# Loading the first block in two parts: sixteen partitions, then the other 112

## Chip, cores, metric

The kernel runs on one core of one Trainium2 chip. The metric is the device time of a run in microseconds. All runs quoted were with a granted clock of 1.0 (full speed).

## The reference

```python
def reference(x):                 # x: float32 [64, 256, 8192], 536.87 MB
    return np.mean(x, axis=2)     # [64, 256]
```

Every element is read once and added once. 16384 means come out.

## The kernel before

The 16384 rows of 32 KB are taken in 64 blocks of 256. Each of the 128 partitions gets two neighbouring rows, so 64 KB of HBM that lie together. From here on, "a row" of a load means these 64 KB of one partition: one DMA engine moves them, and the trace has one record of 65,536 bytes for them. Three slots of SBUF (the core's on-chip memory) hold blocks in turn. SyncE issues all loads, VectorE sums a block. The last block is cut into pieces and shared with ScalarE. The first load's issue is moved by hand ahead of the kernel's opening barrier.

```python
slots = [nc.alloc_sbuf_tensor(f"xt{i}", [P, R, S], F32) for i in range(SLOTS)]   # P=128, R=2, S=8192, SLOTS=3
load_sem = [tc.alloc_semaphore(f"load{i}") for i in range(LOAD_SEMS)]            # 6

def load(dst, src, sem):
    ld = untracked(nc.sync.dma_start(out=dst, in_=src))
    ...
    ld.then_inc(sem, 16)
    return ld

def loaded(n, ins):
    ins._wait_ge(load_sem[n % LOAD_SEMS], 16 * (n // LOAD_SEMS + 1))

for n in range(LB):                       # 63 whole blocks
    xt = slots[n % SLOTS]
    ld = load(xt[:], x_v[n], load_sem[n % LOAD_SEMS])
    if n == 0:
        first = ld
    if n < LB - 1:
        loaded(n, dve_sum(res[:, :, n], xt[:]))
    ...                                   # the last of them is shared with ScalarE
...                                       # last block in pieces, transposes, stores
body_bb.instructions.remove(first.ins)    # the first load goes to the head block,
...                                       # before SyncE's drain
head_bb.instructions.insert(at, first.ins)
```

## Time and profile before

| | before |
|---|---|
| time, median of 5 | 1246.84 us (1246.76 to 1246.90) |
| span of the profiled run | 1245.2 us |
| first sum starts | 21.83 us |
| a block arrives every | 19.35 us |
| VectorE waits before its sums, in total | 153.3 us |
| HBM read over the span | 431 GB/s |

The load stream is the bound: the load queue's records fill 99.8% of the sixteen DMA engines' span, and VectorE waits for each block. The prediction below shows the lines that carry this.

### The profile page before, as it was taken

What the parts mean: (1) busy time and instruction counts of PE and PEld (TensorE: products, weight loads), DVE (VectorE), ACT (ScalarE), POOL (GpSimd) and SP (SyncE); (2) the same over time, 40 slices, a digit from 0 to 9 for tenths busy, and PEclk for the clock granted to TensorE, in tenths of its full rate; (3) what the DMA queues carried; (4) which work ended last, traced back from release to release, by engine and by line L of the source; (5) the groups of instructions that cost most, each with busy time, mean ns of one, the idle gap of its engine ahead of it and who ended that gap; (6) DMA issues with size and microseconds to landing.
All of it is one profiled execution on the core that took longest, in us unless ns stands there. A gap on an engine that the chain in (4) does not pass through costs nothing.

```text
span 1245.2 us, 227 instructions
## 1 busy us (share of the span) xinstructions
PE 0.9 (0%) x2; PEld 0.4 (0%) x2; DVE 1087.4 (87%) x79; ACT 16.5 (1%) x13; POOL 0.7 (0%) x6
## 2 busy tenths in 40 slices
PE   0000000000000000000000000000000000000000
PEld 0000000000000000000000000000000000000000
DVE  3898988989889889898898988989889898898898
ACT  0000000000000000000000000000000000000004
POOL 0000000000000000000000000000000000000000
DMA  9999999999999999999999999999999999999998
GB/s 438 417 425 438 438 438 438 434 408 438 438 438 438 438 438 432 411 438 438 438 438 438 438 415 427 438 438 438 438 438 436 406 438 438 438 438 438 438 429 348
DMA packets 10169, 536.95 MB, mean 431 GB/s; under 512 B 1145, under 2 KB 1464, under 8 KB 1720
## 3 DMA queue, kind: packets, MB, share of 16 engines
q1 hardware_dynamic: 10168, 536.94, 99.8%
q14 instruction: 1, 0.01, 0.0%
HBM read 536.87 MB, written 0.07 MB: 431 GB/s over the span
## 4 chain that ended last, share of the span: by engine, by line
DMA 70%; DVE 29%; SPq 0%; issue 0%; DVEq 0%
DMA xt<-in_x_dram 70%; DVE res L92 29%; DVE fin_in L92 0%; SPq L82 0%; DVE fin_in L98 0%; DVE fin_t L109 0%; DVEq L98 0%
## 5 line engine op out<-in xcount | busy, mean ns | idle before, releaser
L92 DVE TENSOR_REDUCE res<-xt 128x2 f32<-128x16384 f32 (+1 forms) x63 | 1076.4, 17086 | 153.3 <-DMA xt<-in_x_dram 153.3
L95 ACT ACT_TABLE_LOAD x1 | 1.3, 1283 | 1181.3 <-DVE res L92 1181.3
L95 ACT ACTIVATE xt<-xt 128x8192 f32<-128x8192 f32 (+5 forms) x6 | 14.7, 2443 | 43.9 <-DMA xt<-in_x_dram 43.7
L92 DVE TENSOR_REDUCE fin_in<-xt 128x1 f32<-128x256 f32 (+3 forms) x5 | 5.0, 1005 | 0.3 <-DMA xt<-in_x_dram 0.2
L92 DVE TENSOR_REDUCE head<-xt 128x1 f32<-128x4096 f32 x1 | 4.4, 4420 | 0.2 <-DMA xt<-in_x_dram 0.2
L153 PE MATMUL ps<-ident,res 128*63 128x128 f32 x2 | 0.9, 460 | 1230.4 <-ACT xt L95 1229.3
L95 ACT ACTIVATION_READ_ACCUMULATOR xt<-xt 128x1 f32 x6 | 1.1, 186 | 0.0
L72 DVE MEMSET fin<- 128x32 f32 x2 | 0.1, 85 | 0.9 <-PEq L230 0.9
L154 DVE TENSOR_SCALAR bulk<-ps 63x128 f32<-63x128 f32 x2 | 0.6, 278 | 0.4 <-PE ps L153 0.4
L153 PEld LDWEIGHTS ps<-ident,res 128*63 128x63 f32 x2 | 0.4, 180 | 1230.6 <-issue 1229.2
L98 DVE TENSOR_SCALAR_CACHE_REDUCE fin_in<-fin_in 128x265 f32<-128x265 f32 x1 | 0.4, 431 | 0.2 <-DVE fin_in L92 0.2
L109 DVE STREAM_TRANSPOSE fin_t<-fin 128x32 f32<-128x32 f32 x2 | 0.4, 212 | 0.1
L60 POOL TENSOR_SCALAR_AFFINE_SELECT ident<-ident 128x128 f32<-128x128 f32 x1 | 0.3, 295 | 0.1
L98 DVE TENSOR_SCALAR_CACHE_REDUCE head<-head 128x2 f32<-128x2 f32 x1 | 0.2, 156 | 0.1
L59 POOL MEMSET ident<- 128x128 f32 x1 | 0.2, 205 | 0.4 <-POOLq L230 0.4
L230 POOL MEMSET const-bfloat16-1.0<- 128x1 bf16 x1 | 0.1, 103 | 0.0
L230 POOL MEMSET const-uint8-127<- 128x1 uint8 x1 | 0.1, 103 | 0.0
L230 POOL MEMSET const-float32-0.0<- 128x1 f32 x1 | 0.1, 99 | 0.2 <-issue 0.2
L230 POOL MEMSET const-float32-1.0<- 128x1 f32 x1 | 0.1, 99 | 0.0
L98 DVE DVE_READ_ACCUMULATOR head<-head 128x1 f32 x1 | 0.1, 85 | 0.0
L98 DVE DVE_READ_ACCUMULATOR fin_in<-fin_in 128x1 f32 x1 | 0.1, 84 | 0.0
## 6 DMA issues: line engine op xcount, KB each, us to landing
xt<-in_x_dram SPq DMA_DIRECT2D x1, 4096.0 KB, 31.2
xt<-in_x_dram SPq DMA_DIRECT2D x1, 2048.0 KB, 35.7
xt<-in_x_dram SPq DMA_DIRECT2D x1, 1024.0 KB, 37.7
xt<-in_x_dram SPq DMA_DIRECT2D x63, 40.8
xt<-in_x_dram SPq DMA_DIRECT2D x1, 512.0 KB, 38.5
xt<-in_x_dram SPq DMA_DIRECT2D x1, 256.0 KB, 38.7
xt<-in_x_dram SPq DMA_DIRECT2D x1, 128.0 KB, 38.6
fin_in<-in_x_dram SPq DMA_DIRECT2D x1, 128.0 KB, 38.4
```

The costliest lines, as they stand in the source:

```text
L59: nc.gpsimd.memset(ident[:], 0.0)
L60: nc.gpsimd.affine_select(out=ident[:], in_=ident[:], compare_op=mybir.AluOpType.not_equal, fill=1.0, base=0, pattern=[[-1, P]], channel_m ...
L72: nc.vector.memset(fin[r][:], 0.0)
L92: return untracked(nc.vector.tensor_reduce(out=dst, in_=src, axis=X, op=ADD))
L95: return untracked(nc.scalar.activation(out=src, in_=src, func=COPY, accum_out=dst))
L98: return nc.vector.tensor_scalar(out=src, in0=src, scalar1=inv, scalar2=None, op0=mybir.AluOpType.mult, op1=ADD, accum_out=dst,)
L109: nc.vector.transpose(out=fin_t[r][:], in_=fin[r][:])
L153: nc.tensor.transpose(out=ps[:LB, :], in_=res[:, r, :], identity=ident[:])
L154: nc.vector.tensor_scalar_mul(out=bulk[:LB, :, r], in0=ps[:LB, :], scalar1=inv)
L230: nc = _bacc.Bacc("TRN2", target_bir_lowering=False, num_devices=1)
```

## The change

Its intent, a supposition: a first transfer of only sixteen rows (part one) would have one descriptor (an order to move one row) for each engine, so the engines might begin sooner than when 128 descriptors are made. The other 112 rows follow at once in a second transfer (part two).

```diff
+ENGINES = 16
...
     def loaded(n, ins):
-        ins._wait_ge(load_sem[n % LOAD_SEMS], 16 * (n // LOAD_SEMS + 1))
+        loads = n // LOAD_SEMS + 1 + (n % LOAD_SEMS == 0)
+        ins._wait_ge(load_sem[n % LOAD_SEMS], 16 * loads)
...
     for n in range(LB):
         xt = slots[n % SLOTS]
-        ld = load(xt[:], x_v[n], load_sem[n % LOAD_SEMS])
+        sem = load_sem[n % LOAD_SEMS]
         if n == 0:
-            first = ld
+            first = [
+                load(xt[a:b], x_v[n, a:b], sem) for a, b in ((0, ENGINES), (ENGINES, P))
+            ]
+        else:
+            load(xt[:], x_v[n], sem)
...
-    (move first.ins to the head block)
+    for ld in first:
+        (move ld.ins to the head block)
```

The last two hunks are cut: the same lines that moved one issue now move both.

More of the change, by code (lines that the diff above doesn't have):

```diff
@@ L173 @@
     head_bb, body_bb = nc.main_func.blocks[:2]
-    assert first.ins in body_bb.instructions
-    body_bb.instructions.remove(first.ins)
-    at = next(
-        i
-        for i, ins in enumerate(head_bb.instructions)
-        if ins.engine == first.ins.engine and isinstance(ins, mybir.InstDrain)
-    )
-    head_bb.instructions.insert(at, first.ins)
+    for ld in first:
+        assert ld.ins in body_bb.instructions
+        body_bb.instructions.remove(ld.ins)
+        at = next(
+            i
+            for i, ins in enumerate(head_bb.instructions)
+            if ins.engine == ld.ins.engine and isinstance(ins, mybir.InstDrain)
+        )
+        head_bb.instructions.insert(at, ld.ins)
     DVE = mybir.EngineType.DVE
```

## The prediction

> **What bounds the kernel now.** I read the page first: the busy rows by slice, the groups, and the chain that ended last.
>
> ```profile
> DVE  3898988989889889898898988989889898898898
> DMA  9999999999999999999999999999999999999998
> ...
> HBM read 536.87 MB, written 0.07 MB: 431 GB/s over the span
> ...
> DMA xt<-in_x_dram 70%; DVE res L92 29%; DVE fin_in L92 0%; SPq L82 0%; DVE fin_in L98 0%; DVE fin_t L109 0%; DVEq L98 0%
> ...
> L92 DVE TENSOR_REDUCE res<-xt 128x2 f32<-128x16384 f32 (+1 forms) x63 | 1076.4, 17086 | 153.3 <-DMA xt<-in_x_dram 153.3
> ```
>
> The DMA row is full in every slice and moves 431 GB/s on average. VectorE is busy 87%, and all of its idle time before the sums (153.3 us) is ended by a load. The chain gives VectorE 29%, but that is the way slots come free, not the bound. The timeline of VectorE shows it:
>
> ```profile
> 21.83 17.22 DVE L92 TENSOR_REDUCE res<-xt 128x2 f32<-128x16384 f32 x1 [20.80 <-DMA xt<-in_x_dram]
> 41.15 17.22 DVE L92 TENSOR_REDUCE res<-xt 128x2 f32<-128x16384 f32 x1 [2.10 <-DMA xt<-in_x_dram]
> 60.50 17.22 DVE L92 TENSOR_REDUCE res<-xt 128x2 f32<-128x16384 f32 x1 [2.13 <-DMA xt<-in_x_dram]
> ```
>
> A sum takes 17.22 us, a new block lands every 19.35 us (60.50 - 41.15), so VectorE waits 2.1 us each time. A block is 128 rows of 64 KB, 8.39 MB; over 19.35 us that is 433.6 GB/s. Divided over 16 engines, each engine carries 8 rows, one after the other, at 19.35 / 8 = 2.418 us a row; call this one row time. The third slot keeps them supplied: load 3 is issued when the first sum ends (21.83 + 17.22 = 39.05), while load 2 lands only at about 60.5. So there is a reserve of some 20 us, and the time is the sum of each engine's back-to-back rows: whatever delays the slowest engine in the first block moves the end by as much, and nothing later makes it up.
>
> Next the start, in fine windows (columns: window, its length, five engines' busy times, clock, DMA share, GB/s; a packet is counted wholly in the window in which it starts):
>
> ```profile
> 0.00:1.00 1.00, 0.00 (x0) 0.00 (x0) 0.10 (x2) 0.00 (x0) 0.39 (x5) 1.00 0.00 0
> 1.00:1.25 0.25, 0.00 (x0) 0.00 (x0) 0.03 (x1) 0.00 (x0) 0.18 (x2) 1.00 7.85 2621
> 1.25:1.50 0.25, 0.00 (x0) 0.00 (x0) 0.00 (x0) 0.00 (x0) 0.14 (x1) 1.00 3.83 1311
> 1.50:1.75 0.25, 0.00 (x0) 0.00 (x0) 0.00 (x0) 0.00 (x0) 0.00 (x0) 1.00 0.70 262
> 1.75:4.00 2.25, 0.00 (x0) 0.00 (x0) 0.00 (x0) 0.00 (x0) 0.00 (x0) 1.00 0.00 0
> 4.00:4.25 0.25, 0.00 (x0) 0.00 (x0) 0.00 (x0) 0.00 (x0) 0.00 (x0) 1.00 2.42 1049
> 4.25:4.50 0.25, 0.00 (x0) 0.00 (x0) 0.00 (x0) 0.00 (x0) 0.00 (x0) 1.00 6.65 2884
> 4.50:4.75 0.25, 0.00 (x0) 0.00 (x0) 0.00 (x0) 0.00 (x0) 0.00 (x0) 1.00 0.60 262
> ```
>
> 2621 GB/s for 0.25 us is 655 KB, ten rows of 65,536 bytes; then 5, then 1. The sixteen engines start their first rows between 1.0 and 1.75 us after the issue, staggered, and their second rows (4, 11 and 1) between 4.0 and 4.75. This stagger is what the change aims at. In the trace's packet records the first rows start from 1.05 to 1.68 us and end from 4.05 to 4.56; at the end of the run the sixteen parts of a load still land 0.36 us apart, so the stagger is carried to the end.
>
> [...] So 16 rows and 112 rows both use 16 engines, one and seven rows each. [...] all rows of the steady state take the same 2.418 us, 27.1 GB/s an engine. [...]
>
> **The change part by part.** *Added issue.* One more DMA on SyncE's queue; issues of the big loads take 0.33 to 0.44 us in the timeline. The second part is issued about 0.4 us after the first, its rows reach the engines at about 1.5 us, before any first row ends (4.05). Loads 1 and 2 are issued 0.4 us later but are wanted at 21 us. Cost on the path: 0. The waits stay single waits, for 32 instead of 16 on the first; VectorE, ScalarE and TensorE have the same rows in the same order.
>
> *Gain, as intended.* If the stagger comes from 128 descriptors being made one after the other, it shrinks from 0.6 us to about a tenth. At the end only the slowest engine counts, and the sixteen parts land within 0.36 us, so the gain is at most about 0.4 us, 0.03%.
>
> [...]
>
> [...]
>
> Sum for the slowest engine: 3 + 4 = 7 row times, 7 x 2.418 = +16.9 us, minus at most 0.4. Load 0 then lands at 21.8 + 16.9 = 38.7, its sum ends at 55.9 and releases load 3. The fastest engine pays only the 3 row times: it ends load 0 at 28.6 to 29 and runs out of loads 1 and 2 at about 67. So nothing starves, no second cost is added, and the shift is carried unchanged: 1246.84 + 16.9 = 1263.7 us.
>
> **The rivals.** *[...] (load only staggered less).* [...] Time 1246.4 to 1247.5. I give it 15%.
> *[...] only part one pays.* [...] Then only +7.25 us, 1254. I give it 15%.
> *Rows are dealt in turn (row 16 + e + 16j to engine e).* [...] 8 rounds of 4 row times instead of 8 of 1, up to +58 us if engines stay in step, +35 to +55 if they drift apart; around 1290. [...] 15%.
> *The late first block starves the queue.* The reserve of 20 us speaks against: with +16.9 us and engines 10 us apart, 11 us remain.
>
> **Range and chances.** Consecutive sevens get 55%, giving 1259 to 1268[...]. Weighing in the cheaper rivals, which share 30%, I set the point a little below the sum, at 1262.0 us (+1.2%). The range 1246.2 to 1271.0 leaves out the dealing in turn. Within 2% means up to 1271.8: same 0.82; slower 0.17 (the dealing in turn, and a little for worse sharing); faster 0.01, as the intended gain is 0.4 us.
>
> **What would show it.** In the changed kernel's fine windows, sixteen rows should start by about 1.2 us, and the second rows only at about 10 to 11 us: that shows part one. If they start at 4.0 to 4.5, [...] the prediction falls. Load 0 should land at about 38 us, and its parts some 10 us apart (28 to 38) instead of 0.4; [...] over 60 us dealing in turn. From the second block on, VectorE should wait 2.1 us before each sum and blocks should come each 19.35 us as before; a longer period or a changed wait would mean that the cost isn't confined to the first block.

What is cut at the marks said how rows are dealt to engines and which partitions slow one another; no trace of the kernel before showed it. Two terms of the sum are cut with it. The sum came to 7 row times, +16.9 us, so 1263.7 us: +3 row times (7.25 us) on every engine for part one and +4 (9.67 us) on the slowest for part two. "Consecutive sevens" is the supposition that an engine's seven rows of part two go to neighbouring partitions. The first two rivals: that it doesn't matter which partitions a transfer writes, and that part two costs nothing. The 4 row times for sixteen rows that the third rival names were assumed; e3 later measured 3.9.

## More of the kernel before

One more line of the page, the data moved in 40 equal slices of the span, will be compared with the changed kernel's:

```profile
GB/s 438 417 425 438 438 438 438 434 408 438 438 438 438 438 438 432 411 438 438 438 438 438 438 415 427 438 438 438 438 438 436 406 438 438 438 438 438 438 429 348
```

Only the last slice, which holds the tail, is clearly lower. The start costs so little that the first slice reads as full.

## The result

The changed kernel takes 1268.43 us (median of 5, 1267.93 to 1268.69) against 1246.84. The ratio is 1.0172, 95% interval 1.0158 to 1.0186. Ratios here are the mean time of one kernel's fast runs over that of the other's in the same rounds, so not quite the ratio of the medians. The change costs 21.6 us, 1.7%, just inside the 2% that counts as the same.

The page of the changed kernel, in the lines that answer to those of before:

```profile
DVE  0598988988988989889889889898898898898988
DMA  9999999999999999999999999999999999999998
GB/s 217 366 437 430 433 430 430 430 430 433 435 439 441 437 433 430 430 430 430 433 433 433 435 447 435 433 430 430 430 430 433 433 433 433 451 433 433 430 430 338
...
HBM read 536.87 MB, written 0.07 MB: 424 GB/s over the span
...
DMA xt<-in_x_dram 71%; DVE res L94 29%; SPq L83 0%; DVE fin_in L94 0%; DVE fin_in L100 0%; DVE fin_t L111 0%; DVEq L100 0%
...
L94 DVE TENSOR_REDUCE res<-xt 128x2 f32<-128x16384 f32 (+1 forms) x63 | 1076.4, 17086 | 174.4 <-DMA xt<-in_x_dram 174.4
```

The sums cost exactly what they did (1076.4 us). VectorE's wait for loads grew from 153.3 to 174.4 us, by 21.1, nearly the whole loss of 21.6. The loss sits in the first two slices: 217 and 366 GB/s where there were 438 and 417. Note the DMA row: it still shows 9 in those slices. From 15 to 40 us the DMA share is 1.02 (a record counts where it starts) at 252 GB/s; before, from 10 to 20 us, it was 0.97 at 419. So a slow row counts as busy like a fast one, and the DMA row can't tell them apart; the GB/s row can.

VectorE's timeline (start, length, operation, and in brackets the wait and what ended it):

```profile
43.93 17.22 DVE L94 TENSOR_REDUCE res<-xt 128x2 f32<-128x16384 f32 x1 [42.45 <-DMA xt<-in_x_dram]
63.27 17.22 DVE L94 TENSOR_REDUCE res<-xt 128x2 f32<-128x16384 f32 x1 [2.12 <-DMA xt<-in_x_dram]
82.62 17.22 DVE L94 TENSOR_REDUCE res<-xt 128x2 f32<-128x16384 f32 x1 [2.13 <-DMA xt<-in_x_dram]
```

The first sum starts at 43.93 instead of 21.83 us, 22.1 later. After that the rhythm is that of before: 19.35 us a block, a wait of 2.1 us. So one event in the first block moves everything behind it.

The start in fine windows (window, length, five engines' busy times, clock, DMA share, GB/s; a row of 65,536 bytes is counted where it starts):

```profile
1.00:1.25 0.25, 0.00 (x0) 0.00 (x0) 0.00 (x0) 0.00 (x0) 0.00 (x0) 1.00 12.77 1573
1.25:1.50 0.25, 0.00 (x0) 0.00 (x0) 0.12 (x2) 0.00 (x0) 0.20 (x1) 1.00 1.79 262
1.50:1.75 0.25, 0.00 (x0) 0.00 (x0) 0.00 (x0) 0.00 (x0) 0.21 (x1) 1.00 2.10 262
1.75:2.25 0.50, 0.00 (x0) 0.00 (x0) 0.00 (x0) 0.00 (x0) 0.09 (x1) 1.00 8.42 1049
2.25:8.00 5.75, 0.00 (x0) 0.00 (x0) 0.00 (x0) 0.00 (x0) 0.00 (x0) 1.00 0.00 0
8.00:9.00 1.00, 0.00 (x0) 0.00 (x0) 0.00 (x0) 0.00 (x0) 0.00 (x0) 1.00 0.39 66
9.00:10.00 1.00, 0.00 (x0) 0.00 (x0) 0.00 (x0) 0.00 (x0) 0.00 (x0) 1.00 2.51 459
10.00:11.00 1.00, 0.00 (x0) 0.00 (x0) 0.00 (x0) 0.00 (x0) 0.00 (x0) 1.00 2.69 524
```

6, 1, 1 and 8 rows start by 2.25 us; then nothing starts until 8 us, and the second rows (1, 7, 8) come between 8 and 11. Before, they came between 4.0 and 4.75. Two things follow. The first rows take 7.2 to 9.0 us instead of 2.8 to 3.3. And the stagger that the change wanted to shrink did not shrink: the first rows start from 1.03 to 2.05 us, against 1.05 to 1.68 before.

The trace's record of every row shows one DMA engine's work in a chain, as each row starts when the one before it ends. One typical engine and one of the two slowest, in us a row:

```
before, any engine       3.0 | 2.42 2.42 2.42 2.42 2.42 2.42 2.42 | load 1: 2.42 2.42 ...
after, typical engine    8.4 | 5.51 4.79 3.02 3.73 4.41 4.70 4.40 | load 1: 3.26 2.42 ...
after, one of two        8.3 | 5.43 4.79 4.74 3.77 4.55 4.64 4.78 | load 1: 2.77 2.42 ...
```

The first bar ends part one, the second part two. From load 1's second row on all is as before.

### The profile page after: what moved, and what is told of

Same layout as the page of the kernel before. It is cut to its first block, busy times and chain, and to the rows that moved or that the text cites. A ratio compares the mean times of both kernels' runs of the same rounds, so it can differ in the third digit from the quotient of the medians.

```text
span 1266.6 us, 228 instructions
## 1 busy us (share of the span) xinstructions
PE 0.9 (0%) x2; PEld 0.4 (0%) x2; DVE 1087.2 (86%) x79; ACT 16.4 (1%) x13; POOL 0.7 (0%) x6
## 4 chain that ended last, share of the span: by engine, by line
DMA 71%; DVE 29%; SPq 0%; issue 0%; DVEq 0%
DMA xt<-in_x_dram 71%; DVE res L94 29%; SPq L83 0%; DVE fin_in L94 0%; DVE fin_in L100 0%; DVE fin_t L111 0%; DVEq L100 0%
## 5 line engine op out<-in xcount | busy, mean ns | idle before, releaser
L94 DVE TENSOR_REDUCE res<-xt 128x2 f32<-128x16384 f32 (+1 forms) x63 | 1076.4, 17086 | 174.4 <-DMA xt<-in_x_dram 174.4
L97 ACT ACTIVATE xt<-xt 128x8192 f32<-128x8192 f32 (+5 forms) x6 | 14.6, 2441 | 43.9 <-DMA xt<-in_x_dram 43.7
L160 PE MATMUL ps<-ident,res 128*63 128x128 f32 x2 | 0.9, 458 | 1251.9 <-ACT xt L97 1250.8
```

What stands on the lines that cost most here:

```text
L94: return untracked(nc.vector.tensor_reduce(out=dst, in_=src, axis=X, op=ADD))
L97: return untracked(nc.scalar.activation(out=src, in_=src, func=COPY, accum_out=dst))
L160: nc.tensor.transpose(out=ps[:LB, :], in_=res[:, r, :], identity=ident[:])
```

## The experiments

Twelve kernels, all edits of the changed kernel's first block unless told otherwise. Each also has its semaphore count fitted to its number of transfers, which the cuts below leave out. "Loss" is the median less that of the kernel before on the same chip in the same rounds (1246.7 to 1246.9). Each median is of four or five runs, in e11, e12 and e13 of two. The theory that they test: rows written at the same time slow one another or not, depending on which partitions they go to; below, a "conflict" is such a slowing. Where a mark stands before a number and no rival is named, the number is this theory's. The rivals: the splitting itself costs (an issue, descriptors, semaphore increments); the cold start costs; the places in HBM cost.

| run | first block loaded as | time us | loss us | first sum at us |
|---|---|---|---|---|
| e1_columns | 2 x (128 partitions, half the columns) | 1247.00 | 0.2 | 21.82 |
| e2_swap | 112, then 16 | 1268.29 | 21.5 | 43.67 |
| e3_eight_near | 8 x 16 neighbours | 1302.36 | 55.6 | 77.43 |
| e4_eight_spread | 8 x 16, every eighth | 1268.30 | 21.5 | 43.50 |
| e5_halves | 64, then 64 | 1267.96 | 21.3 | 43.31 |
| e11_near_from_spread | e3's partitions, e4's HBM rows | 1302.02 | 55.3 | 77.35 |
| e12_spread_from_near | e4's partitions, e3's HBM rows | 1268.84 | 22.1 | 43.31 |
| e13_wide_pitch | as changed, other HBM pitch | 1268.03 | 21.3 | 43.33 |
| e7_two_foreign | 2 extra rows to partitions 64 and 68, then 128 | 1251.52 | 4.7 | 26.77 |
| e8_two_own | 2 extra rows to partitions 0 and 4, then 128 | 1249.56 | 2.7 | 24.49 |
| e9_extra_16 | 16 extra rows, then 128 | 1255.80 | 9.0 | 31.12 |
| e15_block_30 | 128; block 30 as 16, then 112 | 1269.47 | 22.7 | 21.78 |

Results are correct except in e11, e12 and e13.

### Splitting, or which partitions?

e1_columns splits without breaking up the partitions:

```diff
-load(xt[a:b], x_v[n, a:b], sem) for a, b in ((0, ENGINES), (ENGINES, P))
+load(xt[:, r, :], x_v[n, :, r, :], sem) for r in range(R)
```

> The first block is again loaded in two parts, but each part has all 128 partitions and half of the columns (32 KB a row). [...] 1246.8 us within 0.4, first sum starting at about 22 us. Splitting theory (a second transfer, its descriptors and its semaphore increments cost by themselves): the loss of the change comes again, about 1268.

Measured: ratio 1.0001 (0.9988 to 1.0015). VectorE's timeline is that of before, with the first sum at 21.82:

```profile
21.82 17.22 DVE L94 TENSOR_REDUCE res<-xt 128x2 f32<-128x16384 f32 x1 [20.32 <-DMA xt<-in_x_dram]
41.17 17.22 DVE L94 TENSOR_REDUCE res<-xt 128x2 f32<-128x16384 f32 x1 [2.13 <-DMA xt<-in_x_dram]
```

So a second transfer, twice the records (256 of 32 KB) and 32 increments on the semaphore cost nothing that the runs resolve. The splitting rival falls.

e2_swap keeps the change's two sets and turns their order:

```diff
-... for a, b in ((0, ENGINES), (ENGINES, P))
+... for a, b in ((ENGINES, P), (0, ENGINES))
```

> The same two sets of partitions, the 112 first and the 16 after. [...] the same conflicts in another order, so a loss of 15 to 24 us again (1262 to 1271), the 112 rows taking some 25 to 30 us from the start, and their seven rows seen from a common start. If the loss came from what the 16 rows do at the very start (first descriptors, cold start), the 112 rows would run at about 2.42 us each and the total would stay under 1256.

Measured: 1268.29, ratio 1.0174. The 112 rows run from the start at some 4.6, 4.6, 3.3, 3.1, 4.4, 4.6, 4.5 us a row and their sixteen parts land from 30.1 to 35.0 us, later than the 25 to 30 expected; the 16 rows behind them take 7.2 to 9.2 us each. Both sets are slow wherever they stand.

e3_eight_near and e4_eight_spread use eight transfers of sixteen rows each, so every engine has one row of each transfer, and differ only in which partitions are in one transfer:

```diff
-... for a, b in ((0, ENGINES), (ENGINES, P))
+load(xt[a : a + 16], x_v[n, a : a + 16], sem) for a in range(0, P, 16)     # e3
+load(xt[a:P:8], x_v[n, a:P:8], sem) for a in range(8)                      # e4
```

> The first block in eight transfers of 16 neighbouring partitions, one row for each engine and transfer, so which engine gets which row is not in question up to order. [...] 32 row times of 2.418 us instead of 8, +58 us if the engines stay in step (1305), less, +20 to +58[...]. Splitting theory: seven further transfers at the change's +21.6 for one would be far above that, or a few us if an issue costs only its 0.4 us; and it must equal the run with the spread partitions.

> Eight transfers of 16 rows as in the run with neighbours, but of every eighth partition (0, 8, ..., 120; then 1, 9, ...): same number of transfers, descriptors and increments. [...] 16 row times instead of 8, +19.3 us (about 1266), less if engines drift out of step, and well under the run with neighbours. Splitting theory: the same time as the run with neighbours.

Measured: 1302.36 and 1268.30. In the records each engine's seven rows from the second on take 9.34 to 9.39 us in e3 and 4.94 to 5.11 in e4; counted for all eight, 8 x 9.39 = 75.1 and 8 x 5.11 = 40.9, against 8 x 2.42 = 19.3 in the kernel before, with all 128 partitions in one transfer. That is 3.9 and 2.1 row times for a row; 4 and 2 were expected, and the losses of 55.6 and 21.5 us are near the 58 and 19.3 expected of engines that stay in step. Same number of transfers, 34 us apart: this is the second end of the splitting rival.

### Partitions written, or rows read?

In e3 and e4 the HBM rows are neighbours or every eighth as well. e11 and e12 cross the two sides:

```diff
+load(xt[16 * a : 16 * a + 16], x_v[n, a:P:8], sem) for a in range(8)       # e11
+load(xt[a:P:8], x_v[n, 16 * a : 16 * a + 16], sem) for a in range(8)       # e12
```

> Wrong result on purpose in the first block. Eight transfers of 16 rows to 16 neighbouring partitions, read from every eighth row in HBM. [...] 9.39 us a row and about 1302 us, as with neighbours on both sides. If the places in HBM make it: 5.11 us a row and about 1268, as with every eighth row on both sides.

> Wrong result on purpose in the first block. Eight transfers of 16 rows to every eighth partition, read from 16 neighbouring rows in HBM. [...] 5.11 us a row (or a little less, if the source had a share in it) and about 1268. If the places in HBM make it: 9.39 us a row and about 1302.

Measured: 1302.02 and 1268.84; the first sums of e3, e11, e4 and e12, in this order, each from VectorE's timeline of its kernel:

```profile
77.43 17.22 DVE L94 TENSOR_REDUCE res<-xt 128x2 f32<-128x16384 f32 x1 [73.10 <-DMA xt<-in_x_dram]
```

```profile
77.35 17.22 DVE L94 TENSOR_REDUCE res<-xt 128x2 f32<-128x16384 f32 x1 [72.94 <-DMA xt<-in_x_dram]
```

```profile
43.50 17.22 DVE L94 TENSOR_REDUCE res<-xt 128x2 f32<-128x16384 f32 x1 [37.59 <-DMA xt<-in_x_dram]
```

```profile
43.31 17.22 DVE L94 TENSOR_REDUCE res<-xt 128x2 f32<-128x16384 f32 x1 [37.39 <-DMA xt<-in_x_dram]
```

The time follows the partitions written and not the rows read. The cost is on SBUF's side.

e13_wide_pitch asks the same of the changed kernel itself, whose 112 rows had slowed all engines alike, which my sum did not have:

```diff
+x_w = x_f[0 : 8 * 112].rearrange("(p q) s -> p q s", q=8)[:, 0:R]
-load(xt[a:b], x_v[n, a:b], sem) for a, b in ((0, ENGINES), (ENGINES, P))
+load(xt[0:16], x_v[n, 0:16], sem),
+load(xt[16:P], x_w, sem),
```

> Wrong result on purpose in the first block. The changed kernel, but the 112 rows are read from HBM at a pitch of 256 KB instead of 64 KB; the partitions written are the same. [...] the changed kernel's trace shows all sixteen engines slowed together (rows of 3 to 5 us). If HBM addresses make that, the series of row times (about 5.4, 4.8, 3.1, 3.7, 4.4, 4.7, 4.4 us) changes clearly; if the SBUF side makes it, it stays within 0.3 us each and the time stays at 1268.

Measured: 1268.03. A typical engine's rows of part two are 5.4, 4.7, 3.1, 3.7, 4.4, 4.7, 4.4 us: the series of the changed kernel. HBM's addresses are out.

### How the rows are dealt

```diff
+load(xt[a : a + 64], x_v[n, a : a + 64], sem) for a in (0, 64)             # e5
```

> The first block in two transfers of 64 partitions, four rows for each engine. If the rows of a transfer are dealt in consecutive blocks (four rows an engine)[...]: rows of 4.7 to 5.1 us, as in the run with every eighth partition, and a loss of about 21.5 us again (1268). If they are dealt in turn[...]: rows of 9.4 us and a loss of about 56 us (1302). If conflicts needed different strides, no loss.

Measured: 1267.96, rows of 5.12 us after the first, 4.93 at the change of halves. So 64 neighbouring partitions in one transfer give the row time of every eighth partition (5.11 us, e4) and not that of sixteen neighbours (9.39 us, e3). Time and row time are those expected for rows dealt in consecutive blocks, not those for dealing in turn. But the records don't name partitions: how the rows are dealt was not shown, for 64 as for 112. Of the 112 rows none takes more than 6.2 us, and the seven rows of an engine are not alike. In the changed kernel exactly two engines are slow in the third row, 4.74 and 4.76 us against 2.83 to 3.41 for the other fourteen, and two others in the fourth, 4.40 and 4.68 against 3.67 to 3.77. In the other five rows all sixteen take 4.02 to 6.21 us. The records of e13 and e15 show the same pattern.

### Why all sixteen engines slow down

My sum for part two let most engines run at full rate beside slow ones. e7 and e8, its control, test that. Ahead of a whole first block, two rows go to the third slot (which load 2, held back until they have landed, overwrites). Partitions 64 and 68 were picked to make a conflict, and 0 and 4 to make none; what the choice rested on was not shown, and the runs have to tell:

```diff
+extra_sem = tc.alloc_semaphore("extra")
-load(xt[a:b], x_v[n, a:b], sem) for a, b in ((0, ENGINES), (ENGINES, P))
+load(slots[2][64:69:4], x_v[2, 64:69:4], extra_sem),      # e7: partitions 64, 68
+load(slots[2][0:5:4], x_v[2, 0:5:4], extra_sem),          # e8 instead: partitions 0, 4
+load(xt[:], x_v[n], sem),
...
+            if n == SLOTS - 1:
+                ld._wait_ge(extra_sem, 16)
```

> The whole first block in one transfer of 128 partitions, as in the kernel before, but ahead of it a transfer of two rows (to partitions 64 and 68 of the third slot, overwritten later), so two engines carry one row more[...] four engines are slow in their first row (about 5.1 us instead of 3.0), the other twelve keep about 3.0 us; the end moves by one shared row, about +5.1 us (1251.9). If a conflict slows engines[...], the twelve others show longer first rows too (4 us and more).

> [...] the two extra rows go to partitions 0 and 4[...]. No conflict: two engines carry 9 rows instead of 8 at 2.42 us each, no row is slow, and the end moves by one row, +2.4 us (1249.2). If the extra transfer costs by itself, more than that; if the two rows are on other engines than I think, slow rows show up here and not, or less, in the other run.

Measured: 1251.52 (ratio 1.0038, 1.0024 to 1.0051) and 1249.56 (1.0021, 1.0007 to 1.0035). The times are near the expected 1251.9 and 1249.2, which alone would not show that all engines slow down; the windows do. First e7, then e8 (columns as above):

```profile
1.40:2.60 1.20, 0.00 (x0) 0.00 (x0) 0.12 (x2) 0.00 (x0) 0.50 (x2) 1.00 3.89 874
...
4.00:5.40 1.40, 0.00 (x0) 0.00 (x0) 0.00 (x0) 0.00 (x0) 0.00 (x0) 1.00 0.00 0
5.40:5.80 0.40, 0.00 (x0) 0.00 (x0) 0.00 (x0) 0.00 (x0) 0.00 (x0) 1.00 0.00 0
5.80:7.00 1.20, 0.00 (x0) 0.00 (x0) 0.00 (x0) 0.00 (x0) 0.00 (x0) 1.00 1.92 765
7.00:7.60 0.60, 0.00 (x0) 0.00 (x0) 0.00 (x0) 0.00 (x0) 0.00 (x0) 1.00 0.51 218
```

```profile
1.40:2.60 1.20, 0.00 (x0) 0.00 (x0) 0.12 (x2) 0.00 (x0) 0.50 (x2) 1.00 2.53 874
...
4.00:5.40 1.40, 0.00 (x0) 0.00 (x0) 0.00 (x0) 0.00 (x0) 0.00 (x0) 1.00 1.74 749
```

In both, sixteen rows start between 1.4 and 2.6 us (874 GB/s for 1.2 us is 1.05 MB). In the control all sixteen engines begin their second row between 4.0 and 5.4 us (749 GB/s for 1.4 us). With the two rows on partitions 64 and 68, not one engine does so before 5.8: 14 of the second rows start between 5.8 and 7.0, and 2 between 7.0 and 7.6. In the records the first rows take 4.2 to 5.0 us on every engine, against 2.7 to 3.3 in the control. The kernels differ only in the two rows' partitions and in the HBM rows that are read for them, and e11 and e12 showed that the HBM side doesn't matter (0.3 and 0.5 us). So the places of two rows hold up all sixteen engines, not two or four. In the changed kernel, too, all sixteen are slow in five of part two's seven rows (4.02 us and more); in the third, fourteen keep about 3 us. By what path the two rows hold up the other engines, no run here shows.

### The size of part one

```diff
+load(slots[2][0:16], x_v[2, 0:16], extra_sem),            # e9, else as e7
+load(xt[:], x_v[n], sem),
```

> The part of 16 rows alone: it is loaded as an extra (to partitions 0 to 15 of the third slot, overwritten later), and the first block comes whole in one transfer of 128 partitions behind it. Each engine carries one row more, 2.42 us[...]. By the prediction's term for part one: 4 row times, +9.7 us in all (1256.5), of which 7.25 us are the conflict. By the changed kernel's trace (the last first row ended at 10.6 us there instead of 4.6): about +8.5 us (1255.3). If the changed kernel's loss lay mostly in part one, far more than that, up to +24 us.

Measured: 1255.80, a loss of 9.0 us (ratio 1.0071). An extra row on every engine is 2.42 us of that, so the conflict of the sixteen rows costs 6.5 us. The larger share of the change's loss, 15.1 of 21.6 us by this estimate, is part two's.

### Only at the start?

e15_block_30 moves the two parts from the first block to block 30:

```diff
 if n == 0:
-    first = [load(xt[a:b], x_v[n, a:b], sem) for a, b in ((0, ENGINES), (ENGINES, P))]
+    first = [load(xt[:], x_v[n], sem)]
+elif n == 30:
+    for a, b in ((0, ENGINES), (ENGINES, P)):
+        load(xt[a:b], x_v[n, a:b], sem)
```

> The first block whole again, and block 30 of 63 loaded in the two parts of the change instead, in mid-stream with a full queue ahead of it. [...] about +20 us (1264 to 1269), VectorE waiting once some 20 us longer near the middle and 2.1 us everywhere else; sharing with engines still in block 29 or already in block 31 may move it by some us. If the loss belonged to the cold start, or if a running queue with 20 us in reserve hid it: within 1 us of the kernel before.

Measured: 1269.47, just above the 1264 to 1269 expected; ratio 1.0180. VectorE's timeline around it:

```profile
564.36 17.22 DVE L94 TENSOR_REDUCE res<-xt 128x2 f32<-128x16384 f32 x1 [2.14 <-DMA xt<-in_x_dram]
584.40 17.22 DVE L94 TENSOR_REDUCE res<-xt 128x2 f32<-128x16384 f32 x1 [2.82 <-DMA xt<-in_x_dram]
625.67 17.22 DVE L94 TENSOR_REDUCE res<-xt 128x2 f32<-128x16384 f32 x1 [24.04 <-DMA xt<-in_x_dram]
645.02 17.22 DVE L94 TENSOR_REDUCE res<-xt 128x2 f32<-128x16384 f32 x1 [2.13 <-DMA xt<-in_x_dram]
```

One wait of 24.04 us, 21.9 more than usual, and 0.7 more on the block before (2.82 instead of 2.14); together 22.6, the loss of 22.7. It is no matter of the cold start, and a full queue hides nothing of it.

No run beat the kernel before. e1_columns equals it.

## Why the prediction was right, and where its sizes were off

**The bound.** Right. "Whatever delays the slowest engine in the first block moves the end by as much, and nothing later makes it up": the first sum moved by 22.1 us, the time by 21.6, and the same cut in block 30 costs as much.

**Added issue, cost 0.** Right: e1_columns has it and loses nothing that the runs resolve.

**Gain, as intended, at most 0.4 us.** Not there. The premise that the stagger comes from making 128 descriptors is not borne out: with 16 rows in the first transfer the first starts spread over 1.0 us (e13: 0.6), with 128 over 0.6 (e15: 1.0), so the spread differs as much between kernels with the same first transfer. In e1_columns fifteen engines start between 1.04 and 1.30 us and one at 2.03. What sets the stagger stays open; it was worth too little to follow up.

**Part one, +3 row times, +7.25 us.** Right in kind, a little large: e9 gives 6.5 us. Sixteen neighbouring partitions written at once take 9.39 us a row (e3) where 4 x 2.418 = 9.67 was assumed, and no first row took even that: 7.2 to 9.0 us. In the records the first rows ended from 8.4 to 10.6 us, where the prediction's sign was 10 to 11; the last ended at 10.61 instead of 4.56, 6.1 later.

**Part two, +9.67 us for the slowest and nothing for the fastest.** This is the term of the sum that was mis-sized. The seven rows of a typical engine add up to 30.6 us (5.51 + 4.79 + 3.02 + 3.73 + 4.41 + 4.70 + 4.40) instead of 16.9, so +13.6, and those of the two slowest to 32.5 and 32.7, so +15.6 and +15.8. The step that failed is that some engines slow down and all others keep full speed. e7 shows that the others don't: two rows made all sixteen engines slow (4.2 to 5.0 us against 2.7 to 3.3), and in five of part two's seven rows all sixteen are slow. That also explains why the fastest engine was no better off. The parts of load 0 were to land 10 us apart and landed from 40.6 to 43.9 us, 3.3 apart.

**The sum.** The engine that ended last ended its first row at 10.51 us, 6.0 after the last engine of before (4.56), and its seven rows took 15.6 us more: 21.5, where the first sum moved by 22.1 and the time by 21.6. The prediction had 7.25 + 9.67 = 16.9: one term about 1 us too large, one about 6 too small. Its point of 1262.0 was set lower still to allow for the cheaper rivals, which all failed. The time lies just above the 1259 to 1268 that it gave for consecutive sevens. That the whole range, up to 1271.0, held was partly luck, as the slowing of all sixteen engines was not foreseen.

**Rivals.** That the partitions written don't matter: refuted by e3 against e4 (34 us apart). That only part one pays: refuted by part two's own row times (+13.6 us on a typical engine). Dealing in turn: its times, around 1290 us and 1302 for e5, did not come; how rows are dealt was not shown. A starved queue: the rhythm of 19.35 us from the second block on refutes it, as predicted.

**Left open.** By what path two rows slow all sixteen engines, and why part two's third row slows two engines (4.74 and 4.76 us) and leaves fourteen at 2.83 to 3.41. How 112 rows are dealt to the engines, and which partitions slow one another beyond the sets tried here. Nor did a run look for a cut by partitions that costs nothing.

## What to carry to other kernels

When loads are the bound, don't cut a load of 128 partitions by partitions, not even once: here every cut into fewer partitions cost 21 to 56 us for a single block of 8.4 MB, while a cut by columns cost nothing that the runs resolve (0.2 us, e1). Each engine's rows run back to back, so a loss in one block is paid in full at the end: in e15 it was (22.6 us of waiting, 22.7 of time), with a full queue of three slots. Look at the GB/s row and not at the DMA busy row to see it: in the changed kernel's first slice the one shows 217 instead of 438, the other 9 as ever.
